# Wide matmuls in runs of one width, bank by bank, with other issue points for some transfers: a two-block transformer pass on one core

## The chip, the cores and the metric

The kernel runs on one core of a Trainium2 chip. The time is device microseconds of one launch, the median over several runs. The core has TensorE (PE), VectorE (DVE), ScalarE (ACT) and GpSimd (POOL), and SyncE (SP), which here only issues transfers.

## The reference

One sequence of 256 tokens with 2,048 channels goes through two blocks, in float32. The first has an RG-LRU branch and a sparse-attention branch in parallel, an MLP with squared ReLU and a gated projection of an embedding (PLE). The second has two layers: stick-breaking attention beside gated linear attention, then an S5 state-space mixer with a GLU, each followed by a SwiGLU feed-forward.

```python
y = concatenate([rms_norm(rglru(...)), rms_norm(nsa(...))]); h = h + rms_norm(y @ w_out)
f = square(relu(rms_norm(h) @ mlp_w1)) @ mlp_w2;             h = h + rms_norm(f)
h = h + sigmoid(h @ ple_gate) * (p @ ple_proj)
for layer in range(2):
    y = sb_gla_mixer(...) if layer == 0 else s5_mixer(...)   # s5: gelu(y) @ w_glu, split, val * sigmoid(gate)
    h = h + rms_norm(y)
    gate, up = split(rms_norm(h) @ w_ffn_in[layer]); h = h + rms_norm((silu(gate) * up) @ w_ffn_out[layer])
```

The sparse attention adds a relative position bias that is looked up by the distance of query and key, for 16 heads.

## The kernel before, in words

Activations lie transposed, channels on partitions and 256 tokens (`T`) in the free dimension. Every float32 product is made of three rounded ones: weights and activations are split into a rounded part and a rest (`wh`, `wl`; `X[:, 0]`, `X[:, 1]`), and `wh` times both parts of `X` and `wl` times the first are summed in PSUM.

`wload` (L253 to L263) fetches a weight tile of 512 KB on SyncE's queue into `wr`; ScalarE rounds it to `wh` (L261) and VectorE subtracts to get `wl` (L262). A tile holds two contraction steps `kk` by four output tiles `j` of 128 columns.

`group` (L287 to L322) runs one group: four PSUM banks, one for each `j`, and 8 or more weight tiles. In its **wide** form, each product is a matmul of 512 columns (`wh` with both parts of `X`) and one of 256 (`wl` with the first part), issued by the helper on L304. In its **narrow** form there are three of 256 columns. Stages that are wide: the MLP, the PLE gate, both feed-forwards, the GLU. Narrow ones fill the first block's and the second's mixers. Groups alternate between banks of tag `ps` only and `px, px, ps, ps` (`gpar`). `evac` (L340 to L367) empties a bank: ScalarE copies one half (L357), VectorE adds the other (L361, L364). `pre` is set for the first group of a stage, whose activations are split as it goes (L249).

The order on each engine is set by a list scheduler that goes by program order and priorities; `low(n)` shifts the priority, `issue_after` puts an instruction behind another. Side work comes from generators: `mix_step` takes two steps of `self.mix` after each weight tile in the first block, and `bg_step` takes steps of a background generator in the MLP and layer 0's feed-forward: the S5 tables are made there, much of it on GpSimd. Its `prod` (L1713) makes 32x128 matmuls (L1720), which GpSimd's work on L1762 waits for.

`bias_tables` (L595) makes the 16x511 bias table on TensorE and writes it, skewed, as a [16, 128, 256] tensor `tab` to DRAM, from 16 partitions; `bias_gen` reads it back. `s5` (L1797) loads its tables TB, TT and CBd, and `relay` (L1809) moves the Gelu outputs from one partition layout to another in eight copies per cut, cuts of 8, 4 and 4 column tiles; the issuing engines take turns. The GLU's activations are split from its result (L1948, L1949).

Of the kernel before, what the change touches and what calls it, by code (L numbers as in the profile page):

```python
# [9 lines left out]
F32 = mybir.dt.float32  # L10
# [8 lines left out]
P = 128  # L19
# [38 lines left out]
def layout(inp):  # L58
# [25 lines left out]
    rb = np.zeros((33, 16), np.float32)  # L84
    rb[:32] = g["rel_bias"]
    rb[32] = NEG
    o["relb"] = rb
    dist = np.arange(511) - 255
    b = np.where(dist >= 0, _rel_bucket(dist), 32)
    oh = np.zeros((33, 2, 511), np.float32)  # L90
    oh[b, 0, np.arange(511)] = 1.0
    oh[:, 1] = oh[:, 0, ::-1]
    o["oh"] = oh
    cst = np.zeros((P, 4, P), np.float32)
    cst[:, 0] = np.eye(P)
# [41 lines left out]
class K:  # L137
    def __init__(self, tc, I, out, es, dump=None):
        self.tc, self.nc, self.I, self.out = tc, tc.nc, I, out
        self.es = es  # L140
        self.dumpf = dump
        pool = lambda name, bufs, **k: es.enter_context(tc.tile_pool(name=name, bufs=bufs, **k))
        self.cp = pool("const", 1)
        self.xp = pool("xp", 6)
        self.wp = pool("wp", 4)
        self.ep = pool("ep", 5)
        self.mp = pool("mp", 9)
        self.sp = pool("sp", 4)
# [5 lines left out]
        self.mix, self.mix_n, self.summed = [], 1, None  # L154
        self.hold = ()

    def nm(self, s):
# [95 lines left out]
    def wload(self, pieces, shape=(P, 2, 512)):  # L253

        nc = self.nc
        wr = self.wp.tile(list(shape), F32, tag="wr", name=self.nm("wr"))
        for sl, src in pieces:
            nc.sync.dma_start(wr[sl], src)
# [28 lines left out]
    def group(self, Xk, ks, load, ntile=4, pre=None, narrow=None, tag="ps", kc=2):  # L287

        nc = self.nc
        narrow = not self.alt if narrow is None else narrow
        lhs = lambda w, kk, j: w[:, kk, j * P:(j + 1) * P]
        if narrow:
            banks = [self.ps(tag) for _ in range(ntile // 2)]
            ps = [banks[j // 2][:, (j % 2) * T:(j % 2 + 1) * T] for j in range(ntile)]
        else:
            tags = ["ps"] * 4
            if self.alt:
                self.gpar ^= 1  # L300
                tags = [["ps"] * 4, ["px", "px", "ps", "ps"]][self.gpar]
            ps = [self.ps(tags[j]) for j in range(ntile)]
        n = len(ks)
        mm = lambda o, w, x, a, z: nc.tensor.matmul(o, w, x, start=a, stop=z, skip_group_check=True)  # L304
        for c in range(0, n, kc):
            if pre:
                for k in ks[c:c + kc]:
                    pre(k)
            wh, wl = load(ks[c])
            for kk in range(kc):  # L310
                i = c + kk
                X = Xk(ks[i])
                for j in range(ntile):
                    if narrow:
                        mm(ps[j], lhs(wh, kk, j), X[:, 0], i == 0 and j % 2 == 0, False)
                        mm(ps[j], lhs(wh, kk, j), X[:, 1], False, False)
                        mm(ps[j], lhs(wl, kk, j), X[:, 0], False, i == n - 1)
                    else:
                        mm(ps[j], lhs(wh, kk, j), X, i == 0, False)
                        mm(ps[j][:, 0:T], lhs(wl, kk, j), X[:, 0], False, i == n - 1)  # L320
            self.mix_step()
        return ps  # L322

# [271 lines left out]
    def bias_tables(self):  # L595

        nc, I = self.nc, self.I
        relb = self.m([33, 16], tag="relb", bufs=1)
        nc.scalar.dma_start(relb, I["relb"])
        oh = self.wp.tile([33, 2, 511], F32, tag="wr", name="oh")  # L600
        nc.scalar.dma_start(oh, I["oh"])
        ps = self.ps()
        nc.tensor.matmul(ps[0:16, 0:511], relb, oh[:, 1], start=True, stop=True)
        tb = self.m([16, 512])
        nc.vector.tensor_copy(tb[:, 0:511], ps[0:16, 0:511])
        self.tab = self.dp.tile([16, P, T], F32, tag="tab", name="tab")
        skew = bass.AP(tensor=tb.tensor, offset=tb.offset + 127, ap=[list(tb.ap[0]), [-1, P], [1, T]])
        nc.gpsimd.dma_start(self.tab, skew)


        self.bc = self.c([P, 2, 2, 8, 16], "bc")
        nc.gpsimd.memset(self.bc[:, 0], NEG)
# [11 lines left out]
    def block1_in(self):  # L624
# [36 lines left out]
        with self.tc.issue_after(self.hold[1].ins):  # L661
            L = self.lru_open(UG)
        cmp_ = {}
        self.mix, self.mix_n = [self.compress_gen(kk, cmp_), self.bias_gen(), self.lru_gen(L)], 2

        sl = lambda a, b: (slice(None), slice(None), slice(a, b))
        ps = self.group(Xk, ks, lambda k0: self.wload([(sl(0, 256), self.wsrc(W, k0, C_KS, 2, 256)),
# [385 lines left out]
    def block1(self):  # L1053
# [24 lines left out]
            ld(k)  # L1078
        self.upd = self.post_norm(Y, acc)
        self.mlp()  # L1080
        self.ple()
        self.dump("h3", self.h)

# [387 lines left out]
    def ffn(self, layer):  # L1471
        nc, I = self.nc, self.I
        V, S = nc.vector, nc.scalar
        X, pre = self.make_x(("ng2", layer * 64 + 32))
        rb = self.rtile("a")
        W1, W2 = I["w_ffn_in_2"][layer], I["w_ffn_out_2"][layer]
        Y = self.newY()
# [41 lines left out]
    def s5_gen(self):  # L1519
# [193 lines left out]
        def prod():  # L1713

            k, cx, bt = pend
            kt = self.ps()
            for i in range(2):
                for r in range(4):
                    q = 2 * r + i
                    nc.tensor.matmul(kt[r * 32:r * 32 + 32, 0:P], bt[:, i, r * 32:r * 32 + 32],  # L1720
                                     cx[q // 4][:, q % 4].rearrange("p t h -> p (t h)"), start=(i == 0), stop=(i == 1),
                                     skip_group_check=True)
# [74 lines left out]
    def s5(self):  # L1797
        nc, I = self.nc, self.I
        V, S = nc.vector, nc.scalar

        TB = [self.xs([P, 4, 2, 16, 32], F32) for _ in range(2)]
        for kp in range(8):
            nc.sync.dma_start(TB[kp // 4][:, kp % 4], self.TBd[kp])
        U = self.xs([P, 8, NK, 32], F32)
        Us = self.xs([P, 8, NK, 32], F32)
        fl = lambda a: a.rearrange("p g k c -> p g (k c)")
# [117 lines left out]
        def outer(kp):  # L1924
# [83 lines left out]
```

## Time and profile before

| | us |
|---|---|
| median of 3 runs | 3652.32 (3651.43 to 3671.67) |
| profiled execution, device time | 3657.45 |
| its span, first to last instruction | 3655.6 |
| TensorE busy | 3501.3 |
| stages by the profile: first mixer | 0 to 449 |
| MLP | 449 to 1205 |
| PLE and second block's first mixer | 1205 to 1750 |
| feed-forward, layer 0 | 1750 to 2590 |
| S5 | 2590 to 2688 |
| GLU | 2688 to 2874 |
| feed-forward, layer 1 | 2882 to 3655 |

Times in the rows below are from the start of the span. A row of a timeline is: start, duration, engine, line, operation, output and inputs, and in brackets how long the engine was idle before it and what ended that. Matmuls are pipelined: their durations overlap, and the distance from start to start is what one costs.

### The profile page before, as it was taken

To read this page: it belongs to the slowest core of one execution; us is meant where nothing else is said; L and a number is where in the kernel's file an instruction comes from. 1 tells how busy PE (TensorE), PEld (TensorE's weight loads), DVE (VectorE), ACT (ScalarE), POOL (GpSimd) and SP (SyncE) were. 2 spreads that over 40 slices of the span, in tenths; PEclk is the share of its full clock that TensorE was granted. 3 is DMA by queue.
4 is the path that set the end of the run, shared out by engine and by line. 5 is a ranking of instruction groups with operands and counts; after the bars stand their busy time and mean duration, and the time that the engine had idled before them with its cause. 6 is when DMAs were issued, how large, how long until landed. Compare 5 with 4: busy or idle time off the path is not lost. (4 is left out here: it accounts for less than half of the span.)

```text
span 3655.6 us, 59158 instructions
## 1 busy us (share of the span) xinstructions
PE 3501.3 (96%) x22198; PEld 3060.9 (84%) x22198; DVE 2353.4 (64%) x3610; ACT 1833.1 (50%) x2879; POOL 1022.5 (28%) x1498
## 2 busy tenths in 40 slices
PE   8989999999999999999899999999779999999998
PEld 8888888888888898999787888887668888888887
DVE  6686785567656866546765566566755765555566
ACT  4656654644445654346644444344555544444444
POOL 1231242299620112104334555465400200000000
PEclk9999999999999999999999999999989999999999
DMA  8644456667765564565567776677875466665663
GB/s 216 207 130 151 130 172 189 181 210 211 229 202 187 180 198 135 149 194 187 161 207 227 225 228 211 212 225 246 261 219 185 144 192 188 190 187 188 187 187 127
DMA packets 506551, 699.60 MB, mean 191 GB/s; under 512 B 43239, under 2 KB 317671, under 8 KB 506264
## 3 DMA queue, kind: packets, MB, share of 16 engines
q1 hardware_dynamic: 472848, 628.60, 55.8%
q0 software_dynamic: 27120, 63.05, 5.8%
q10 hardware_dynamic: 6296, 4.17, 0.4%
q8 instruction: 174, 2.85, 0.3%
q14 instruction: 113, 0.93, 0.1%
HBM read 654.22 MB, written 37.22 MB: 189 GB/s over the span
## 5 line engine op out<-in xcount | busy, mean ns | idle before, releaser
L304 PE MATMUL ps<-x,wh 128*128 128x512 f32 (+1 forms) x8560 | 2498.4, 355 | 62.1 <-DVE e L361 19.3
L262 DVE TENSOR_TENSOR wl<-wr,wh 128x1024 fp32r<-128x1024 f32 x1126 | 1441.4, 1285 | 1099.6 <-ACT wh L261 1095.3
L304 PE MATMUL ps<-x,wl 128*128 128x256 f32 x6832 | 1922.4, 283 | 0.8 <-DVE wl L262 0.8
L261 ACT ACTIVATE wh<-wr 128x1024 fp32r<-128x1024 f32 x1126 | 1184.0, 1057 | 1245.0 <-PE ps L304 1051.9
L304 PEld LDWEIGHTS ps<-x,wh 128*128 128x128 f32 x8560 | 1510.7, 191 | 319.5 <-issue 30.3
L304 PEld LDWEIGHTS ps<-x,wl 128*128 128x128 f32 x6832 | 1306.1, 191 | 11.1 <-issue 5.6
L304 PE MATMUL px<-x,wh 128*128 128x512 f32 (+1 forms) x1776 | 658.3, 396 | 11.2 <-DVE x L249 6.8
L304 PE MATMUL px<-x,wl 128*128 128x256 f32 x1744 | 491.7, 282 | 0.5 <-DVE wl L262 0.5
L304 PEld LDWEIGHTS px<-x,wh 128*128 128x128 f32 x1776 | 332.6, 189 | 94.4 <-DVE x L249 8.6
L304 PEld LDWEIGHTS px<-x,wl 128*128 128x128 f32 x1744 | 330.5, 190 | 4.8 <-issue 3.2
L527 POOL TENSOR_TENSOR e<-x,r_c 128x256 f32<-128x256 f32 x40 | 39.8, 1001 | 1051.0 <-DVE r_c L448 1042.8
L357 ACT ACTIVATE e<-ps 128x256 f32<-128x256 f32 x324 | 120.5, 377 | 75.2 <-PE ps L304 63.4
L1762 POOL TENSOR_TENSOR m<-m,m 128x128 f32<-128x128 f32 x128 | 70.3, 573 | 302.5 <-PE pm L1720 302.5
L376 POOL TENSOR_TENSOR acc<-acc,sq 128x256 f32<-128x256 f32 x89 | 78.0, 876 | 252.7 <-ACT sq L375 250.0
L245 ACT ACTIVATE x<-e 128x256 fp32r<-128x256 f32 x168 | 68.2, 411 | 90.1 <-DVE e L1500 47.3
L246 DVE TENSOR_TENSOR x<-e,x 128x256 fp32r<-128x256 f32 x168 | 86.0, 521 | 26.4 <-ACT x L245 22.6
L1761 POOL TENSOR_TENSOR m<-m,m 128x128 f32<-128x128 f32 x128 | 82.7, 671 | 0.7
L1779 POOL TENSOR_TENSOR m<-m,m 128x256 f32<-128x256 f32 x64 | 59.6, 932 | 71.7 <-DMA m<-in_s5bT_dram 71.0
L361 DVE TENSOR_TENSOR e<-ps,e 128x256 f32<-128x256 f32 x168 | 69.9, 416 | 6.4 <-ACT e L357 6.4
L1780 POOL TENSOR_TENSOR m<-m,m 128x256 f32<-128x256 f32 x64 | 73.7, 1152 | 0.1
L738 PE MATMUL ps<-wh,x 128*128 128x512 f32 x160 | 64.6, 404 | 0.0
L740 PE MATMUL ps<-wh,x 128*128 128x512 f32 x160 | 63.2, 395 | 0.0
(488 smaller groups left out, 2895.3 us busy)
## 6 DMA issues: line engine op xcount, KB each, us to landing
wr<-in_w_ffn_in_dram SPq DMA_DIRECT2D x704, 256.0 KB, 3.3
wr<-in_mlp_w_dram SPq DMA_DIRECT2D x256, 512.0 KB, 4.2
wr<-in_w_ffn_out_dram SPq DMA_DIRECT2D x176, 512.0 KB, 4.3
wr<-in_w_in_dram SPq DMA_DIRECT2D x152, 512.0 KB, 3.8
wr<-in_w_out_dram SPq DMA_DIRECT2D x64, 512.0 KB, 4.1
wr<-in_w_glu_dram SPq DMA_DIRECT2D x128, 256.0 KB, 3.1
wr<-in_ple_gate_dram SPq DMA_DIRECT2D x32, 512.0 KB, 4.5
wr<-in_w_in_dram SPq DMA_DIRECT2D x32, 256.0 KB, 4.9
```

Source lines behind the costliest of these rows:

```text
L245: a = nc.scalar.activation(dst[:, 0], src, AF.Copy)
L246: b = (eng or nc.vector).tensor_tensor(dst[:, 1], src, dst[:, 0].bitcast(F32), op=ALU.subtract)
L261: nc.scalar.activation(wh, wr, AF.Copy)
L262: nc.vector.tensor_tensor(wl, wr, wh.bitcast(F32), op=ALU.subtract)
L304: mm = lambda o, w, x, a, z: nc.tensor.matmul(o, w, x, start=a, stop=z, skip_group_check=True)
L357: a = S.activation(t, ps[:, T:2 * T], AF.Copy)
L361: self.hold = a, V.tensor_tensor(y, ps[:, 0:T], t, op=ALU.add)
L376: (eng or nc.vector).tensor_tensor(acc, acc, q, op=ALU.add)
L738: nc.tensor.matmul(ps, xh, wh, start=first, stop=False, skip_group_check=True)
L1761: G_.tensor_tensor(cx[:, q], u_(0), l_(0), op=ALU.mult)
L1762: G_.tensor_tensor(t1[:, q], u_(1), l_(1), op=ALU.mult)
L1780: G_.tensor_tensor(t1, v4(gb[0][:, 1]), v4(gb[1][:, 1 - ri]), op=ALU.mult)
```

## The change

Five things change. First, `group` goes through a weight tile bank by bank (all `kk` of one `j`, then the next `j`; in a first group only its last tile) and, where it is wide, takes the products in runs: up to `self.run` matmuls with `wh`, then as many with `wl`. `self.run` is 8 up to the end of the MLP, 2 from the PLE gate through layer 0's feed-forward and the GLU, 4 in layer 1's feed-forward. Second, the bias table is made on 128 partitions (eight copies of the 16 heads) and written in eight pieces, each of 16 rows from another 16 partitions; the pieces come from a generator at the head of `self.mix`, and the table's one-hot matrix no longer lies in a weight buffer. Third, `prod`'s matmuls get a higher priority. Fourth, the S5 tables TB and two of TT are loaded in between or behind the last 25 weight loads ahead of S5. Fifth, the relay of the Gelu outputs is issued by GpSimd alone for the first cut, by GpSimd and SyncE for the other two, where GpSimd and ScalarE (and SyncE in the last) took turns.

```diff
-    o["relb"] = rb
+    o["relb"] = np.tile(rb, (1, 8))
-    oh = np.zeros((33, 2, 511), np.float32)
+    oh = np.zeros((33, 512), np.float32)
...
+        self.run = 8
...
             wh, wl = load(ks[c])
-            for kk in range(kc):
-                i = c + kk
-                X = Xk(ks[i])
-                for j in range(ntile):
-                    if narrow:
...
-                    else:
-                        mm(ps[j], lhs(wh, kk, j), X, i == 0, False)
-                        mm(ps[j][:, 0:T], lhs(wl, kk, j), X[:, 0], False, i == n - 1)
+            order = [(kk, j) for j in range(ntile) for kk in range(kc)]
+            if pre and c + kc < n:
+                order = [(kk, j) for kk in range(kc) for j in range(ntile)]
+            runs = 1 if narrow else self.run
+            for r in range(0, len(order), runs):
+                for part in range(2):
+                    for kk, j in order[r:r + runs]:
...
+                        elif part == 0:
+                            mm(ps[j], lhs(wh, kk, j), X, i == 0, False)
+                        else:
+                            mm(ps[j][:, 0:T], lhs(wl, kk, j), X[:, 0], False, i == n - 1)
...
-        relb = self.m([33, 16], tag="relb", bufs=1)
+        relb, oh = self.m([33, P], tag="relb", bufs=1), self.m([33, 512])
-        oh = self.wp.tile([33, 2, 511], F32, tag="wr", name="oh")
...
-        skew = bass.AP(tensor=tb.tensor, offset=tb.offset + 127, ap=[list(tb.ap[0]), [-1, P], [1, T]])
-        nc.gpsimd.dma_start(self.tab, skew)
+        def gen():
+
+            for r in range(8):
+                rows = tb[r * 16:r * 16 + 16]
+                nc.gpsimd.dma_start(self.tab[:, r * 16:r * 16 + 16], bass.AP(
+                    tensor=rows.tensor, offset=rows.offset + 127 - 16 * r, ap=[list(rows.ap[0]), [-1, 16], [1, T]]))
+                yield 1
+
+        self.tab_gen = gen()
...
-        self.mix, self.mix_n = [self.compress_gen(kk, cmp_), self.bias_gen(), self.lru_gen(L)], 2
+        self.mix, self.mix_n = [self.tab_gen, self.compress_gen(kk, cmp_), self.bias_gen(), self.lru_gen(L)], 2
...
         self.mlp()
+        self.run = 2
         self.ple()
...
+        self.run = (2, 4)[layer]
...
+            with self.low(-self.bg_low):
+                for i in range(2):
+                    for r in range(4):
+                        q = 2 * r + i
+                        nc.tensor.matmul(kt[r * 32:r * 32 + 32, 0:P], bt[:, i, r * 32:r * 32 + 32],
...
+        late = self.loads[-25:]
         for kp in range(8):
-            nc.sync.dma_start(TB[kp // 4][:, kp % 4], self.TBd[kp])
+            with self.tc.issue_after(late[3 * kp].ins):
+                nc.sync.dma_start(TB[kp // 4][:, kp % 4], self.TBd[kp])
...
-                nc.sync.dma_start(tl[:, i], tt_src(len(tts)))
+                with self.tc.issue_after(late[-1].ins):
+                    nc.sync.dma_start(tl[:, i], tt_src(len(tts)))
...
-                    relay(Yg, Yt, k0, k1, (nc.gpsimd, nc.scalar) if i < 2 else (nc.gpsimd, nc.scalar, nc.sync))
+                    relay(Yg, Yt, k0, k1, (nc.gpsimd, nc.sync) if i else (nc.gpsimd,))
```

On TensorE in layer 0's feed-forward (one weight tile, `wh_19239` with its rest; four banks) the order before is:

```order
L304 MATMUL px_19140<-x_18755,wh_19239 128x512
L304 MATMUL px_19140<-x_18755,wl_19240 128x256
L304 MATMUL px_19141<-x_18755,wh_19239 128x512
L304 MATMUL px_19141<-x_18755,wl_19240 128x256
L304 MATMUL ps_19142<-x_18755,wh_19239 128x512
L304 MATMUL ps_19142<-x_18755,wl_19240 128x256
L304 MATMUL ps_19143<-x_18755,wh_19239 128x512
L304 MATMUL ps_19143<-x_18755,wl_19240 128x256
L304 MATMUL px_19140<-x_18755,wh_19239 128x512
L304 MATMUL px_19140<-x_18755,wl_19240 128x256
L304 MATMUL px_19141<-x_18755,wh_19239 128x512
```

and after the change, for the same tile, which is now called `wh_19246` (x2 stands for the two contraction steps):

```order
L305 MATMUL px_19147<-x_18762,wh_19246 128x512 x2
L305 MATMUL px_19147<-x_18762,wl_19247 128x256 x2
L305 MATMUL px_19148<-x_18762,wh_19246 128x512 x2
L305 MATMUL px_19148<-x_18762,wl_19247 128x256 x2
L305 MATMUL ps_19149<-x_18762,wh_19246 128x512 x2
L305 MATMUL ps_19149<-x_18762,wl_19247 128x256 x2
L305 MATMUL ps_19150<-x_18762,wh_19246 128x512 x2
L305 MATMUL ps_19150<-x_18762,wl_19247 128x256 x2
L305 MATMUL px_19147<-x_18762,wh_19269 128x512 x2
L305 MATMUL px_19147<-x_18762,wl_19270 128x256 x2
```

The two contraction steps of a bank now stand together, two of 512 columns and then two of 256; the fourth bank is reached after six pairs of the tile and no longer after three. In the MLP all eight `wh` products of a tile stand ahead of its eight `wl` products.

On SyncE, at the end of S5, where the last CBd loads (L1794), the relay's copies (L1812, `x<-x`) and the GLU's weight loads (L258) meet, the order before is:

```order
L1794 DMA wl_27933<-CBd 128x1024
L1794 DMA wr_27943<-CBd 128x1024
L258 DMA wr_27980<-in_w_glu_dram 128x2x256 x2
L258 DMA wr_28007<-in_w_glu_dram 128x2x256 x2
L258 DMA wr_28034<-in_w_glu_dram 128x2x256 x2
L258 DMA wr_28061<-in_w_glu_dram 128x2x256
L1812 DMA x_27572<-x_27571 128x1x128 x2
L258 DMA wr_28061<-in_w_glu_dram 128x2x256
```

and after the change (L1812, L1832 and L259 are the same lines):

```order
L1812 DMA wl_27940<-CBd 128x1024
L1832 DMA x_27579<-x_27578 128x1x128 x4
L1812 DMA wr_27950<-CBd 128x1024
L259 DMA wr_27987<-in_w_glu_dram 128x2x256 x2
L259 DMA wr_28014<-in_w_glu_dram 128x2x256 x2
L259 DMA wr_28041<-in_w_glu_dram 128x2x256 x2
L259 DMA wr_28068<-in_w_glu_dram 128x2x256
L1832 DMA x_27579<-x_27578 128x1x128 x4
L259 DMA wr_28068<-in_w_glu_dram 128x2x256
```

Four copies have come in ahead of the last CBd load and four among the GLU's weight loads, where two stood before; ScalarE had eleven such copies and has none now.

## Rows read from the trace of the kernel before

**Rows 1.** the page: busy time of the engines; shares of the last chain

```profile
PE 3501.3 (96%) x22198; PEld 3060.9 (84%) x22198; DVE 2353.4 (64%) x3610; ACT 1833.1 (50%) x2879; POOL 1022.5 (28%) x1498
...
PE 36%; DVE 3%; DMA 2%; ACT 1%; issue 1%; POOL 0%; ACTq 0%; SPq 0%; DVEq 0%; POOLq 0%
```

**Rows 2.** TensorE's groups by shape: count, busy us, mean ns, idle before

```profile
L304 PE MATMUL ps<-x,wh 128*128 128x512 f32 x5104 | 1853.4, 400 | 46.6 <-DVE e L361 19.3 <-DVE x L249 13.7 <-DVE x L361 6.3
L304 PE MATMUL px<-x,wh 128*128 128x512 f32 x1712 | 646.8, 400 | 11.2 <-DVE x L249 6.8 <-ACT wh L261 2.6 <-DVE x L1949 1.8
```

**Rows 3.** windows, line 304 alone: length, PE busy (count), PEld, clock, DMA, GB/s

```profile
2950.00:3600.00 650.00, 650.00 (x3709) 565.95 (x3708) 1.00 0.61 188
3100.00:3200.00 100.00, 100.00 (x577) 87.51 (x577) 1.00 0.61 189
```

**Rows 4.** TensorE's waits over the span: us in total, times, longest

```profile
PE ps L304 <- DVE e L361: 19.3, 14, 2.9
PE ps L304 <- ACT wh L261: 14.1, 4, 7.5
```

**Rows 5.** timeline of TensorE, second mixer, 512 columns behind 512

```profile
1555.05 0.39 PE L740 MATMUL ps<-wh,x 128*128 128x512 f32 x1
...
1562.30 0.39 PE L739 MATMUL ps<-wl,x 128*128 128x512 f32 x1
```

**Rows 6.** timeline of TensorE, first mixer, narrow triples of 256 columns

```profile
60.04 0.28 PE L304 MATMUL ps<-x,wl 128*128 128x256 f32 x1
...
60.40 0.28 PE L304 MATMUL ps<-x,wl 128*128 128x256 f32 x1
```

**Rows 7.** timeline of TensorE, second mixer, 256 columns, weights of 16 columns

```profile
1371.75 0.28 PE L728 MATMUL ps<-x,wl 128*16 128x256 f32 x1
...
1372.09 0.28 PE L728 MATMUL ps<-x,wl 128*16 128x256 f32 x1
```

**Rows 8.** the page's costliest groups: a weight load, and VectorE's subtraction

```profile
L262 DVE TENSOR_TENSOR wl<-wr,wh 128x1024 fp32r<-128x1024 f32 x1126 | 1441.4, 1285 | 1099.6 <-ACT wh L261 1095.3
...
L304 PEld LDWEIGHTS ps<-x,wl 128*128 128x128 f32 x6832 | 1306.1, 191 | 11.1 <-issue 5.6
```

**Rows 9.** TensorE's waits in layer 0's feed-forward, 1760 to 2590 us

```profile
PE ps L304 <- DVE e L361: 11.8, 6, 2.9
...
PE ps L304 <- DVE x L361: 4.9, 4, 2.0
PE ps L304 <- DVE e L364: 4.8, 3, 3.4
```

**Rows 10.** TensorE's waits in the MLP, 460 to 1205 us

```profile
PE ps L304 <- DVE e L361: 7.5, 8, 1.9
```

**Rows 11.** timelines of VectorE and TensorE in layer 0's feed-forward

```profile
2250.69 3.56 DVE L262 TENSOR_TENSOR wl<-wr,wh 128x1024 fp32r<-128x1024 f32 x1 [0.43 <-ACT wh L261]
...
2256.75 0.79 PE L304 MATMUL ps<-x,wh 128*128 128x512 f32 x1 [2.52 <-DVE e L361]
```

**Rows 12.** window of all engines there; the clock follows POOL

```profile
2256.00:2260.00 4.00, 3.25 (x10) 2.78 (x11) 2.43 (x6) 2.39 (x4) 3.48 (x6) 0.57 0.52 183
```

**Rows 13.** transfers issued from 55 to 100 us: count, KB, us to landing

```profile
tab<-m POOLq DMA_DIRECT2D x1, 2048.0 KB, 25.5
wr<-in_w_in_dram SPq DMA_DIRECT2D x8, 256.0 KB, 14.4
```

**Rows 14.** timeline of TensorE, first mixer and end of S5

```profile
84.77 0.58 PE L304 MATMUL ps<-x,wh 128*128 128x256 f32 x1 [5.73 <-ACT wh L261]
...
2680.07 1.08 PE L1847 MATMUL px<-wl,x 128*32 128x128 f32 x16 [5.15 <-DMA wl<-CBd]
```

**Rows 15.** timeline of ScalarE, end of S5

```profile
2673.69 7.88 ACTq L1812 DMA_DIRECT2D x<-x  x4
2681.61 0.60 ACT L1930 ACTIVATE x<-pm 128x512 f32<-128x512 f32 x1 [7.95 <-DMA x<-x]
```

**Rows 16.** GpSimd's waits over the span

```profile
POOL m L1762 <- PE pm L1720: 302.5, 12, 86.8
```

More of the change, by code (lines that the diff above doesn't have):

```diff
@@ L86, in layout @@
     rb[32] = NEG
-    o["relb"] = rb
+    o["relb"] = np.tile(rb, (1, 8))
     dist = np.arange(511) - 255
     b = np.where(dist >= 0, _rel_bucket(dist), 32)
-    oh = np.zeros((33, 2, 511), np.float32)
-    oh[b, 0, np.arange(511)] = 1.0
-    oh[:, 1] = oh[:, 0, ::-1]
+    oh = np.zeros((33, 512), np.float32)
+    oh[b, 510 - np.arange(511)] = 1.0
     o["oh"] = oh
@@ L154, in __init__ @@
         self.mix, self.mix_n, self.summed = [], 1, None
+        self.loads = []
+        self.run = 8
         self.hold = ()
@@ L257, in wload @@
         for sl, src in pieces:
-            nc.sync.dma_start(wr[sl], src)
+            self.loads.append(nc.sync.dma_start(wr[sl], src))
         wh = self.wp.tile(list(shape), F32R, tag="wh", name=self.nm("wh"))
@@ L309, in group @@
             wh, wl = load(ks[c])
-            for kk in range(kc):
-                i = c + kk
-                X = Xk(ks[i])
-                for j in range(ntile):
-                    if narrow:
-                        mm(ps[j], lhs(wh, kk, j), X[:, 0], i == 0 and j % 2 == 0, False)
-                        mm(ps[j], lhs(wh, kk, j), X[:, 1], False, False)
-                        mm(ps[j], lhs(wl, kk, j), X[:, 0], False, i == n - 1)
-                    else:
-                        mm(ps[j], lhs(wh, kk, j), X, i == 0, False)
-                        mm(ps[j][:, 0:T], lhs(wl, kk, j), X[:, 0], False, i == n - 1)
+            order = [(kk, j) for j in range(ntile) for kk in range(kc)]
[5 more added lines that the diff above has]
+                    for kk, j in order[r:r + runs]:
+                        i = c + kk
+                        X = Xk(ks[i])
+                        if narrow and part == 0:
+                            mm(ps[j], lhs(wh, kk, j), X[:, 0], i == 0 and j % 2 == 0, False)
+                            mm(ps[j], lhs(wh, kk, j), X[:, 1], False, False)
+                        elif narrow:
+                            mm(ps[j], lhs(wl, kk, j), X[:, 0], False, i == n - 1)
+                        elif part == 0:
+                            mm(ps[j], lhs(wh, kk, j), X, i == 0, False)
+                        else:
+                            mm(ps[j][:, 0:T], lhs(wl, kk, j), X[:, 0], False, i == n - 1)
             self.mix_step()
@@ L597, in bias_tables @@
         nc, I = self.nc, self.I
-        relb = self.m([33, 16], tag="relb", bufs=1)
+        relb, oh = self.m([33, P], tag="relb", bufs=1), self.m([33, 512])
         nc.scalar.dma_start(relb, I["relb"])
-        oh = self.wp.tile([33, 2, 511], F32, tag="wr", name="oh")
         nc.scalar.dma_start(oh, I["oh"])
         ps = self.ps()
-        nc.tensor.matmul(ps[0:16, 0:511], relb, oh[:, 1], start=True, stop=True)
-        tb = self.m([16, 512])
-        nc.vector.tensor_copy(tb[:, 0:511], ps[0:16, 0:511])
+        nc.tensor.matmul(ps, relb, oh, start=True, stop=True)
+        tb = self.m([P, 512])
+        nc.vector.tensor_copy(tb, ps)
         self.tab = self.dp.tile([16, P, T], F32, tag="tab", name="tab")
-        skew = bass.AP(tensor=tb.tensor, offset=tb.offset + 127, ap=[list(tb.ap[0]), [-1, P], [1, T]])
-        nc.gpsimd.dma_start(self.tab, skew)
+        def gen():
[5 more added lines that the diff above has]
+        self.tab_gen = gen()
         self.bc = self.c([P, 2, 2, 8, 16], "bc")
@@ L1716, in prod @@
             kt = self.ps()
[L1717 to L1722, printed above, removed]
+            with self.low(-self.bg_low):
[3 more added lines that the diff above has]
+                        nc.tensor.matmul(kt[r * 32:r * 32 + 32, 0:P], bt[:, i, r * 32:r * 32 + 32],
+                                         cx[q // 4][:, q % 4].rearrange("p t h -> p (t h)"), start=(i == 0), stop=(i == 1),
+                                         skip_group_check=True)
             kp = self.m([P, 240])
```

## The prediction

> **What bounds the kernel now.** I read the page first: TensorE is busy 96% of the span, 3501 us, and the chain that ended last is TensorE's more than any other engine's [rows 1]. So the time is TensorE's instruction stream plus its holes, and a change counts only if it shortens the one or closes the other. I then asked four things of the trace: how long one product takes when nothing waits, who TensorE waits for, what happened in the largest holes, and what clock it got there.
>
> The stream is 6,816 wide pairs: a 512-column matmul with the rounded weights `wh`, then a 256-column one with their rests `wl` [rows 2]. From 2950 to 3600 us TensorE issues 3,709 line-304 matmuls in 650 us at full granted clock and without a hole: 350.5 ns a pair. In the best 100 us it is 577, or 346.6 ns a pair [rows 3]. The span holds 154 us in which TensorE is idle (3655.6 - 3501.3). The largest entries in its list of waits are VectorE's evacuation (`e L361`, 19.3 us in 14 waits) and late `wh` tiles (14.1 us in 4) [rows 4].
>
> The profiled execution has a span of 3655.6 us and took 3657.45 us by the device clock; the median of the runs is 3652.32. The sum is made against 3657.45; I carry its difference over to the median.
>
> **1. Wide products in runs.** The arithmetic stays, only the order within one weight tile changes (8 pairs a tile): eight `wh` then eight `wl` up to the end of the MLP, two and two through the gate projection, layer 0's feed-forward and the GLU, four and four in layer 1. What does a matmul cost behind one of its own width? 512 behind 512, each with its own weights: 32 instructions from 1555.05 to 1562.30 us, 226.6 ns each [rows 5]. 256 behind 256, each with its own 128-column weights: three in 0.36 us, 120 ns each [rows 6]. Together 346.6 ns, the same as the best alternating stretch. So alternation costs on average 350.5 - 346.6 = 3.9 ns a pair, and I book it to the two changes of width in a pair. A run of r keeps one of r: it saves 7/8, 1/2, 3/4 of it. By the counts in the program's order there are 1,984 pairs at r=8, 2,768 at r=2 and 2,064 at r=4: 1,736 + 1,384 + 1,548 = 4,668 pairs saved, times 3.9 ns = **-18 us**.
>
> Bounds. Not all width changes need cost something: the alternation itself drops to 346.6, so 0 is possible. Below that, 256-column matmuls with 16-column weights go at 0.34 us for three, 113.3 ns [rows 7]; if runs did that with 128-column weights, the pair saves 10.6 ns: -49 us. I do not take it, since the full-sized row is the nearer one. Above: a weight load's own record lasts 191 ns [rows 8]; were a `wl` run held to that, a pair would take 226.6 + 191 = 418 ns. The 120 ns are of this very matmul with such loads, so I stay with it and treat the rest as a rival below.
>
> [...]
>
> **2. Banks free sooner, needed sooner.** The new order goes bank by bank within a weight tile, where the old one visited all four banks for each contraction step. At the end of a group the first bank's last product therefore lies further ahead of the group's end: 1.04 us before, 0.72 at r=8, 2.08 at r=2, 1.62 at r=4 (the products that follow it, at the durations above). Evacuation can start 1 us sooner in layer 0's feed-forward. Against it, the next group reaches its third bank no earlier than before (0.9 us before, about 1.4 to 1.6 after, by position) and its fourth 0.1 to 0.6 us earlier. There TensorE waits 11.8 + 4.8 + 4.9 us for evacuations [rows 9]. [...] The 13 waits lose 0.4 to 0.9 us each where they are as long, some 6 us, and I add 3 us for half-clock spells that no longer follow: **-9 us**. Bounds: all 21.5 us and the spells, -28; or +8, if the fourth bank is now what is late. In the MLP they are 7.5 us [rows 10]; there r=8 frees the first bank later, not sooner, and the third is needed 0.2 us later: **-1** (-5..+5). Layer 1 has hardly any.
>
> **3. The bias table.** One 2 MB write from 16 partitions takes 25.5 us; beside it eight weight loads of 256 KB take 14.4 us each [rows 13], ScalarE has no tile to round, and TensorE stands still for 5.73 us [rows 14]. The change writes the same bytes in eight pieces from 16 partitions each; GpSimd issues the eight with nothing between them. Each piece still reads 16 partitions, so the crowding may last as long; what is sure is that the table's source no longer holds a weight buffer. The hole and as much clock as the stall above lost are some 8 us, and smaller holes follow: bounds 0 to -15, nearer 0 because bytes and queue stay: **-3**. The compression's matmuls and the gate work move back in this block by about 96 matmuls; they cover one another, 0 (-10..+10).
>
> **4. Relays of the S5 output.** Before, ScalarE issued half of them itself: it stood 7.88 us in one batch, and the next Gelu waited 7.95 us [rows 15]. TensorE meanwhile waited 5.15 us for CBd [rows 14]. Now GpSimd and SyncE issue them. The stall goes to SyncE: its four copies wait for the sixth Gelu and stand ahead of the last CBd load, and the GLU's weight loads are queued behind that. That Gelu is no longer held, so I put the CBd load at about its old time and the last Gelus some 3 us sooner: **-3** (-8..+3).
>
> **5. At nothing.** The `prod` matmuls (line 1720) stand some 14 us earlier in TensorE's queue; GpSimd waited 302.5 us in 12 waits for their results [rows 16], 25 us in the mean, and TensorE's list of waits has no entry for that line: GpSimd's inputs lie ready far ahead, and 14 us fit in. Were that cover gone, each of 32 rounds would hold TensorE for the missing time. The loads of TB and `ttq` are spread over, or put behind, the last weight loads of layer 0; what they take from the queue is the same bytes, read only by S5 behind that stage.
>
> **Sum:** -18 - 9 - 1 - 3 - 3 = -34: 3657.45 - 34 = 3623 by a profile like this one, **3619 us** in the terms of the median (3652.3 - 34, rounded up).
>
> **Rivals.** *The runs gain nothing* and only the holes shrink: -16, 3636 us. For it: the alternation reaches 346.6 by itself in places. Against: it does so rarely, the mean over 650 us is 350.5.
> *More than one hole closes at once:* 256-runs towards 113 ns (-30 rather than -18), the feed-forward's stalls gone (-21) and the table's hole with its clock (-10): 3652 - 61 = 3591. For it: each term's bound is a row; against: VectorE's 3.56 us operation and the table's bytes stay.
> *Weight loads set the pace of the `wl` runs.* In alternation a short matmul is followed by a long one, beside which a load has time; eight short ones in a row have none, and its record lasts 191 ns [rows 8]. The run loses from 124 ns a `wl` matmul on (350.5 - 226.6), and the kernel becomes slower by over 1% from 135 ns (36.5 us and the other terms' 16 over 4,668 pairs are 11 ns more). At 140 ns: 4,668 x 16 ns = +75, less 16: 3711 us. Against it: the narrow triples load weights for every matmul and go at 120 ns.
> [...]
>
> **Chances.** Sum as made, 3603 to 3634: 50%. More holes, below 3603: 19%, and the bare rate 1%. Runs gain nothing, 3634 to 3660: 23%. Weight loads or a new wait, above 3660: 7%, most of it above 3689. A measurement here tells about 1%, 36.5 us, from no change, so faster is below 3616: 20 plus 17 of the forecast's 50, 37%; slower 5%; within 1%: 58%. The range of 3585 to 3652 leaves out some 3% below and 15% above.
>
> **What would show it.** Step 1: line-304 matmuls in 3000 to 3100 us rising above 573, in the MLP most; like-after-like at 226 and 120. Step 2: `e L361`, `e L364` and `x L361` in layer 0's feed-forward falling from 21.5 us to about 15. Step 3: the 5.73 us hole. Step 4: no ScalarE wait for `x<-x`, and a GLU that starts 3 us sooner after the feed-forward. It is wrong if runs keep 350 ns a pair, or if the fourth bank or GpSimd's products become TensorE's wait.

## The result, and the profile after

The changed kernel takes 3609.95 us in the median, the kernel before 3654.62 beside it: the ratio is 0.9871, with a 95% interval of 0.9831 to 0.9911. The forecast was 3619 within 3585 to 3652. The profiled execution took 3605.78 us (before 3657.45); the page says of it, in the form of [rows 1]:

```profile
PE 3475.6 (96%) x22198; PEld 3054.7 (85%) x22198; DVE 2336.3 (65%) x3610; ACT 1829.6 (51%) x2880; POOL 1024.9 (28%) x1510
...
PE 82%; DVE 7%; issue 3%; ACT 3%; DMA 2%; POOL 2%; SPq 0%; ACTq 0%; DVEq 0%; POOLq 0%
```

TensorE's busy time fell by 26 us and its idle time from 154 to 128 us. Where the time went is seen by stage. I take a wide stage from the start of its first 512-column product to that of its last, by count, so that both traces are cut at the same instruction; the first mixer is what lies ahead of the MLP. Us by the profiles:

| stage | before | after | difference | forecast |
|---|---|---|---|---|
| first mixer | 449.2 | 437.1 | -12.1 | -3 |
| MLP | 741.2 | 735.7 | -5.6 | -8 |
| feed-forward, layer 0 | 804.2 | 772.7 | -31.5 | -13 |
| between it and the GLU (S5) | 124.8 | 123.6 | -1.2 | -3 |
| GLU | 160.6 | 157.2 | -3.4 | -1 |
| feed-forward, layer 1 | 732.6 | 735.3 | +2.7 | -6 |
| all else | 643.0 | 642.4 | -0.6 | -1 |

So the total came out near the forecast, from other terms. Layer 0's feed-forward gave more than twice its share, the first mixer four times, and layer 1, which should have gained 6 us, gained nothing (before + prod, below, has its old code and takes 735.2 there). TensorE's waits in layer 0's feed-forward (those of [rows 9]; L369 and L372 are the old L361 and L364):

```profile
PE ps L305 <- DVE x L250: 6.9, 6, 1.8
PE ps L305 <- ACT x L548: 2.4, 1, 2.4
PE ps L305 <- DVE x L369: 2.0, 1, 2.0
PE ps L305 <- DVE e L372: 1.1, 1, 1.1
...
PE ps L305 <- DVE e L369: 1.0, 4, 0.4
```

The three entries of evacuation are 4.1 us where they were 21.5. The table's write and the weight loads beside it, in the form of [rows 13]:

```profile
wr<-in_w_in_dram SPq DMA_DIRECT2D x16, 256.0 KB, 5.4
...
tab<-m POOLq DMA_DIRECT2D x8, 256.0 KB, 10.1
```

A weight load beside the write lands after 5.4 us where it was 14.4, and the hole of 5.73 us [rows 14] has no successor. The pair's cost in layer 1, in the form of [rows 3]:

```profile
2900.00:3550.00 650.00, 649.97 (x3698) 565.87 (x3697) 1.00 0.60 187
```

3,698 matmuls in 650 us are 351.5 ns a pair, where it was 350.5.

### The profile page after: what moved, and what is told of

It reads as the page before. It is cut to its first block, busy times and chain, and to the rows that moved or that the text cites. A ratio compares the mean times of both kernels' runs of the same rounds, so it can differ in the third digit from the quotient of the medians.

```text
span 3604.0 us, 59118 instructions
## 1 busy us (share of the span) xinstructions
PE 3475.6 (96%) x22198; PEld 3054.7 (85%) x22198; DVE 2336.3 (65%) x3610; ACT 1829.6 (51%) x2880; POOL 1024.9 (28%) x1510
## 4 chain that ended last, share of the span: by engine, by line
PE 82%; DVE 7%; issue 3%; ACT 3%; DMA 2%; POOL 2%; SPq 0%; ACTq 0%; DVEq 0%; POOLq 0%
PE ps L305 60%; PE px L305 15%; DVE wl L263 1%; ACT wh L262 1%; DVE x L536 1%; PE ps L753 1%; PE ps L755 1%; PE ps L754 1%; PE pm L1738 1%; DVE e L535 1%; DVE x L250 1%; POOL acc L384 0%; DMA wr<-in_w_in_dram 0%; PE px L975 0%; DMA m<-in_wg_dram 0%
## 5 line engine op out<-in xcount | busy, mean ns | idle before, releaser
L305 PE MATMUL ps<-x,wh 128*128 128x512 f32 (+1 forms) x8560 | 2135.8, 354 | 40.7 <-DVE x L250 15.3
L305 PEld LDWEIGHTS ps<-x,wh 128*128 128x128 f32 x8560 | 1395.0, 191 | 149.2 <-issue 18.0
L305 PE MATMUL ps<-x,wl 128*128 128x256 f32 x6832 | 1387.8, 283 | 0.0
L305 PEld LDWEIGHTS ps<-x,wl 128*128 128x128 f32 x6832 | 1182.5, 191 | 147.0 <-issue 2.4
L305 PE MATMUL px<-x,wh 128*128 128x512 f32 (+1 forms) x1776 | 523.0, 395 | 12.9 <-DVE x L250 7.3
L305 PEld LDWEIGHTS px<-x,wl 128*128 128x128 f32 x1744 | 295.1, 190 | 54.2 <-issue 2.6
L305 PEld LDWEIGHTS px<-x,wh 128*128 128x128 f32 x1776 | 291.1, 190 | 41.8 <-DVE x L250 8.6
L305 PE MATMUL px<-x,wl 128*128 128x256 f32 x1744 | 313.8, 282 | 0.0
L369 DVE TENSOR_TENSOR e<-ps,e 128x256 f32<-128x256 f32 x168 | 69.8, 417 | 2.9 <-ACT e L365 2.9
L753 PE MATMUL ps<-wh,x 128*128 128x512 f32 x160 | 64.1, 400 | 0.1
L754 PE MATMUL ps<-wl,x 128*128 128x512 f32 x160 | 62.6, 391 | 0.8 <-DVE wl L263 0.8
```

What stands on the lines that cost most here:

```text
L753: nc.tensor.matmul(ps, xh, wh, start=first, stop=False, skip_group_check=True)
L754: nc.tensor.matmul(ps, xh, wl, start=False, stop=False, skip_group_check=True)
```

## The experiments

Theory A was the prediction's own: the bank order frees banks sooner. The rivals: the runs did it (B), or the side work of S5 (C), which I had put at nothing. Most runs undo or change one thing in the changed kernel; one adds one thing to the kernel before; the last two move `prod` in the kernel with runs of 2. Us by stage from each profile, and medians:

| kernel | first mixer | MLP | layer 0 | GLU | layer 1 | median | ratio to before (95%) |
|---|---|---|---|---|---|---|---|
| before | 449.2 | 741.2 | 804.2 | 160.6 | 732.6 | 3654.62 | 1 |
| changed | 437.1 | 735.7 | 772.7 | 157.2 | 735.3 | 3609.95 | 0.9871 (0.9831 to 0.9911) |
| runs of 1 | 438.1 | 740.5 | 779.3 | 160.3 | 734.2 | 3618.98 | 0.9912 (0.9884 to 0.9940) |
| runs of 2 | 435.5 | 730.2 | 769.5 | 157.2 | 729.0 | 3592.04 | 0.9845 (0.9813 to 0.9877) |
| old bank order | 434.9 | 732.6 | 774.9 | 158.5 | 735.2 | 3611.03 | 0.9889 (0.9864 to 0.9915) |
| old side work | 437.8 | 739.4 | 803.9 | 158.6 | 735.9 | 3646.24 | 0.9988 (0.9965 to 1.0010) |
| old prod | 438.4 | 740.1 | 811.9 | 157.7 | 735.5 | 3645.59 | 0.9964 (0.9950 to 0.9978) |
| old TB, TT | 445.0 | 737.3 | 776.6 | 158.7 | 735.7 | 3619.56 | 0.9886 (0.9863 to 0.9909) |
| old table | 448.0 | 735.3 | 769.1 | 157.7 | 735.4 | 3613.87 | 0.9875 (0.9855 to 0.9895) |
| runs by part | 438.6 | 733.5 | 769.8 | 157.6 | 733.1 | 3602.75 | 0.9846 (0.9818 to 0.9874) |
| before + prod | 449.5 | 737.9 | 780.3 | 160.1 | 735.2 | 3629.21 | 0.9916 (0.9900 to 0.9932) |
| runs of 2, prod at 60 | 436.6 | 728.8 | 786.4 | 157.2 | 728.9 | 3607.61 | 0.9864 (0.9848 to 0.9879) |
| runs of 2, prod at 20 | 437.9 | 735.4 | 806.6 | 157.7 | 728.9 | 3637.32 | 0.9936 (0.9911 to 0.9960) |

The runs stand in four groups, each beside its own runs of before; a stage's time repeats within about 4 us where its code is the same, except the first mixer, which takes 434.9 to 445.0 with the new table. What moves it is mostly the granted clock: its mean in the mixer was 0.954 where it took 445.0 and 0.973 in the changed kernel, which is 20.5 and 11.9 us lost (the stage's time, times one less the mean).

**Runs of 1.** `self.run` is 1 throughout; the bank order stays.

```diff
-        self.run = 8
+        self.run = 1
```

> The changed kernel with runs of 1 in every wide stage: the bank-by-bank order within a weight tile stays, wh and wl alternate again. In the changed kernel's trace a pair costs 348.4 to 348.6 ns in layer 0's feed-forward and in the GLU (runs of 2), 349.6 in the MLP (8), 350.5 in layer 1 (4); before it was 351.4, 350.2 and 350.1. Theory A (the bank order closed layer 0's stalls, the runs of 2 gave only the pair's 2.9 ns): layer 0's feed-forward 773 + 6 = 779 us with evacuation waits as low as now (4 us), layer 1 unchanged within 2 us, total about 3617 us. Theory B (the runs closed the stalls): evacuation waits of layer 0 back at 20 us, feed-forward near 800 us, total 3640. Theory C (side transfers and the prod matmuls closed them): as A.

Layer 0 went to 779.3 as A and C had it, not to 800, with 3 us of evacuation waits: the runs had not closed the stalls. The runs as chosen gave some 9 us by the medians, 12 by the profiles.

**Runs of 2.** The same throughout with 2.

```diff
-        self.run = 8
+        self.run = 2
```

> The changed kernel with runs of 2 in every wide stage. If a run of 2 is what costs least per pair (348.5 ns) and frees the first bank 2.1 us ahead of the group's end everywhere: the MLP loses 1,984 x 1.1 = 2 us and most of its 8.4 us of evacuation waits, layer 1 2,064 x 2 = 4 us: total about 3600 us. Rival (the pair's cost goes by what else the core does in a stage, not by the run's length): MLP and layer 1 keep 349.6 and 350.5 ns a pair, only the MLP's waits fall: 3605 us.

3592 us, below both 3600 and 3605, 27 less than runs of 1 in the same group, and the best of all kernels here. MLP and layer 1 both gained, so the length matters and 2 is better than 4 or 8. The pair in layer 1, first with runs of 1, then of 2 (351.3 and 348.8 ns):

```profile
2910.00:3560.00 650.00, 649.94 (x3701) 565.54 (x3700) 1.00 0.59 187
```

```profile
2885.00:3535.00 650.00, 649.95 (x3727) 567.61 (x3726) 1.00 0.59 189
```

**Old bank order, new runs.** In the wide groups alone; the narrow ones keep the new order.

```diff
-            if pre and c + kc < n:
+            if not narrow or pre and c + kc < n:
                 order = [(kk, j) for kk in range(kc) for j in range(ntile)]
```

> The changed kernel with the old visiting order of the banks within a weight tile (contraction step by contraction step) and the new run lengths. Theory A (bank order closed the stalls of layer 0): evacuation waits there return towards 21 us, its feed-forward to 795 us or more, total about 3635 us. Theory C (side work): waits stay near 4 us, feed-forward 773 us, total 3610. In the MLP the order of a run of 8 changes only the wl half, so no more than 3 us either way.

Layer 0 took 774.9, 2 us more than changed; theory A falls.

**Old side work.** `prod` without its raised priority, the loads of TB and TT as before.

```diff
-            with self.low(-self.bg_low):
...
-            with self.tc.issue_after(late[3 * kp].ins):
-                nc.sync.dma_start(TB[kp // 4][:, kp % 4], self.TBd[kp])
+            nc.sync.dma_start(TB[kp // 4][:, kp % 4], self.TBd[kp])
...
-                with self.tc.issue_after(late[-1].ins):
```

> The changed kernel with the S5 side work as before: prod matmuls at their old priority, the loads of TB and of two TT tiles at their old places. Theory C: layer 0's feed-forward back towards 795 us and its evacuation waits towards 21 us, total about 3632 us. Theory A: feed-forward 773 to 777 us, total 3610 to 3615; GpSimd's waits for line 1720 back from 245 to 300 us without cost.

Layer 0 went back to 803.9, further than expected, and the total to 0.9988 of before: theory C holds, and in this kernel the side work carries nearly all of the gain. The next two split it.

**Old prod alone, then old TB and TT alone.** The two halves of the edit above; the first is

```diff
-            with self.low(-self.bg_low):
-                for i in range(2):
+            for i in range(2):
```

> The changed kernel with prod's matmuls at their old priority; TB and the two TT tiles loaded at the new places. With all three undone, layer 0's feed-forward went back from 773 to 804 us. Theory C1 (prod's place in TensorE's queue shifts GpSimd's rounds against VectorE's wl subtractions): feed-forward 798 to 806 us, some 22 VectorE subtractions over 2.5 us there (9 in the changed kernel), total about 3638 us. Theory C2 (the loads of TT, which wait on SyncE for TTd, hold up the weights): feed-forward 773 to 778, total about 3612 us.

> The changed kernel with the loads of TB and the two TT tiles at their old places, prod's matmuls at the new priority: the complement of the run before. C1: feed-forward 773 to 778 us, total 3610 to 3615 us. C2: 798 to 806 us, total about 3638.

811.9 and 776.6: it is `prod`. The 22 stretched subtractions that C1 expected did not come: over 2.5 us there are 7 in layer 0 with old `prod` and 5 in the changed kernel. The evacuation waits in layer 0, with old `prod`:

```profile
PE ps L305 <- DVE e L369: 16.2, 8, 3.1
...
PE ps L305 <- DVE x L369: 4.8, 3, 2.1
PE ps L305 <- DVE e L372: 1.6, 1, 1.6
```

and with old TB and TT:

```profile
PE ps L305 <- DVE e L372: 5.1, 3, 2.9
PE ps L305 <- DVE x L369: 2.6, 1, 2.6
PE ps L305 <- DVE e L369: 0.7, 2, 0.4
```

The second kernel's median is 10 us above changed, of which layer 0 shows 4; its first mixer, with the same code, is 8 us longer (by the clock, as above), and the intervals of the two ratios overlap, so what the moved loads are worth is not settled.

**Before, with the new place of prod alone.** The edit above, the other way round, in the kernel before.

> The kernel before with one edit: prod's matmuls at the new priority. In TensorE's order they then stand at the first pair of a group of 64 (in layer 0's feed-forward), before at the 41st. Theory C1: GpSimd waits for them and then works some 15 us; from the 41st pair that stretch lies over the group's end, where VectorE must evacuate, from the first pair it ends before it. Then this edit alone takes layer 0's feed-forward from 804 to 775 us or so and its evacuation waits from 21 to under 6 us, total about 3622 us. If it needs the bank order too: feed-forward 785 to 800, total 3635 to 3650.

Layer 0 fell from 804.2 to 780.3 and the whole by 30 us (0.9916), a little short of the expected 775 and 3622, with 8.4 us of evacuation waits where under 6 were expected. The edit is enough by itself:

```profile
PE ps L304 <- DVE e L364: 4.5, 4, 2.3
PE ps L304 <- DVE x L361: 3.3, 2, 2.6
...
PE ps L304 <- DVE e L361: 0.6, 2, 0.4
```

**Prod at pair 60 and at pair 20 of 64.** Changed, runs of 2 throughout, and in the first kernel (half as much delay again as in the kernel before, 150 for 100)

```diff
-            with self.low(-self.bg_low):
+            with self.low(self.bg_low // 2):
```

and `-self.bg_low // 2` in the second (half of the old delay).

> The changed kernel with runs of 2 everywhere (3592 us, layer 0's feed-forward 769.5) and prod's matmuls at half the old delay: in most groups they stand at pair 60 of 64. C1: GpSimd's first additions fall on the group's end, 1.4 us behind, so evacuation waits come back, 12 to 20 us, feed-forward 785 to 800, total 3608 to 3623. If only 'earlier than the 41st pair' counts, or the group's end is not what matters: below 775 and 3598.

> As the run before, but prod's matmuls at half the new advance: they stand at pair 20 of 64, and the group's end is 15 us behind, where GpSimd's stretch fades out. C1: waits between the two, 5 to 12 us, feed-forward 772 to 785, total 3595 to 3608. If earlier is all that counts: as pair 0 or 40 by half, 786.

Pair 60 gave 786.4, in the expected range, with 11.5 us of waits, a little under the 12 to 20 expected. Pair 20 gave 806.6 and 23.5 us of waits, as bad as pair 40, where I had expected the middle (5 to 12 us of waits). The waits, for pair 60 and for pair 20:

```profile
PE ps L305 <- DVE e L369: 7.1, 10, 1.2
...
PE ps L305 <- DVE e L372: 4.2, 5, 2.3
...
PE ps L305 <- DVE x L369: 0.2, 1, 0.2
```

```profile
PE ps L305 <- DVE e L369: 12.9, 13, 2.2
PE ps L305 <- DVE e L372: 6.3, 4, 4.9
...
PE ps L305 <- DVE x L369: 4.3, 3, 1.9
```

So it is not how early `prod` comes, and theory C1 as I had it is not the whole either. Layer 0 in parts, us, from the traces: TensorE's idle time, what the granted clock takes (as above), and what the 12 products of `prod` in this stage take of TensorE's stream (first to last of their matmuls, less the wide pairs between; before + prod has one product at a clock of 0.59):

| kernel | layer 0 | idle | clock | `prod` itself |
|---|---|---|---|---|
| before | 804.2 | 26.8 | 8.5 | 37.2 |
| before + prod | 780.3 | 13.0 | 5.1 | 35.8 |
| changed | 772.7 | 10.8 | 5.1 | 33.1 |
| old prod | 811.9 | 34.2 | 18.8 | 37.3 |
| runs of 2 | 769.5 | 11.0 | 1.7 | 33.1 |
| runs of 2, prod at 60 | 786.4 | 16.7 | 1.7 | 40.8 |
| runs of 2, prod at 20 | 806.6 | 25.8 | 1.7 | 50.0 |

The first way in which the place acts is `prod` itself. A product is sixteen matmuls, which the scheduler puts between the wide ones in up to eight places (here for pair 20):

```profile
2347.64 0.41 PE L1736 MATMUL pm<-m,m 128*32 128x128 f32 x2
2347.97 0.39 PE L305 MATMUL ps<-x,wl 128*128 128x256 f32 x1
2348.20 0.40 PE L305 MATMUL ps<-x,wh 128*128 128x512 f32 x1
2348.53 0.41 PE L1736 MATMUL pm<-m,m 128*32 128x128 f32 x2
2348.86 0.50 PE L305 MATMUL ps<-x,wh 128*128 128x512 f32 x1
```

A product costs 4.17 us in eight places, 3.12 in six, 2.58 in five and 1.72 in three, about 0.5 us a place. At pair 20 all twelve stand in eight places, at the first pair in five or six. Of the 37 us that pair 20 loses against runs of 2, 17 are this, and of the 17 us at pair 60, 8; of the 39 us of old `prod` only 4. So pair 60's 786.4 was in the range partly by luck.

The second way is GpSimd, which waits for `prod` and then works. With old `prod`, at the 41st pair of a group (the start, the end of a first stretch of arithmetic, and the start of a second):

```profile
2234.96 1.53 POOL L1779 TENSOR_TENSOR m<-m,m 128x128 f32<-128x128 f32 x4 [28.23 <-PE pm L1737]
...
2259.90 0.76 POOL L1798 TENSOR_TENSOR m<-m,m 128x256 f32<-128x256 f32 x1
...
2270.93 0.76 POOL L1763 TENSOR_TENSOR m<-m,s5rp 128x128 f32<-128x128 f32 x2 [8.52 <-DMA m<-in_s5cb_dram]
```

and in the changed kernel, at the first:

```profile
2196.01 1.85 POOL L1780 TENSOR_TENSOR m<-m,m 128x128 f32<-128x128 f32 x4 [26.55 <-PE pm L1738]
...
2221.01 0.86 POOL L1799 TENSOR_TENSOR m<-m,m 128x256 f32<-128x256 f32 x1
...
2229.80 0.97 POOL L1764 TENSOR_TENSOR m<-m,s5rp 128x128 f32<-128x128 f32 x2 [6.01 <-DMA m<-in_s5cb_dram]
```

Additions and multiplications go on for 26 us behind the product; GpSimd then waits 6 to 9 us for its next loads and works again from some 34 to 44 us behind it. The next two group ends come some 8 and 30 us behind a product at the 41st pair, 14 and 37 behind one at pair 20, at once and 22 behind one at pair 60, and 21.5 and 44 behind one at the first pair, where both stretches are running out. Beside GpSimd's arithmetic VectorE's `wl` subtractions stretch: in layer 0 of the kernel before, the 136 `wl` subtractions without any such work over them take 1.21 to 1.23 us, the 121 others 1.53 us in the mean and up to 3.57 [rows 11]; why they stretch, no run shows. The evacuations themselves (L361, L364) take 0.41 to 0.43 us in any case; they stand behind those.

That is most of it in the kernel before, where 13.0 of 20.3 us of evacuation waits (counted up to layer 0's last 512-column product) stand within 20 us behind a product. It is not with old `prod` in the changed kernel (8.8 of 22.7), nor at pair 20 (4.0 of 18.6) or pair 60 (2.8 of 11.2): there most waits stand at the second group end. With old `prod` and at pair 20 half of all the waits or more, 13.2 and 9.3 us, come within 7 us behind a wait of ScalarE for a late weight load. With old `prod`:

```profile
2393.16 1.06 ACT L262 ACTIVATE wh<-wr 128x1024 fp32r<-128x1024 f32 x1 [2.67 <-DMA wr<-in_w_ffn_in_dram]
...
2398.11 0.73 PE L305 MATMUL ps<-x,wh 128*128 128x512 f32 x2 [2.93 <-DVE e L369]
```

No VectorE operation of the 9 us before this wait is stretched by over 0.3 us; ScalarE's part of the evacuation stands behind the late rounding, and ahead of that GpSimd's own loads and stores run, with the DMA engines busy throughout (a share of 1.03 to 1.05 from 2386 to 2390 us). In the changed kernel ScalarE waits 21.7 us for weight loads in layer 0 too, but none of these waits lies within 7 us ahead of an evacuation wait. So the single edits show that the place of `prod` decides; that it does so by where GpSimd's round (arithmetic and transfers) meets the groups' ends fits the traces at all four places; how much of the waits goes by stretched VectorE operations and how much by late loads, no run separates.

**Old table.** The table made and written as before.

```diff
-        relb, oh = self.m([33, P], tag="relb", bufs=1), self.m([33, 512])
+        oh = self.wp.tile([33, 2, 511], F32, tag="wr", name="oh")
...
+        nc.gpsimd.dma_start(self.tab, skew)
```

> The changed kernel with the bias table made and written as before (one write of 2 MB from 16 partitions, the one-hot matrix in a weight buffer). The first mixer took 449.2 us before and 437.1 in the changed kernel. If the write crowds the weight loads: a hole of 4 to 6 us near 85 us and half clock behind it, mixer back at 447 to 450, total 3620 to 3622. Rival (the other order of tiles, compression and gates made the 12 us): mixer stays at 437 to 440, total 3610.

The first mixer is back at 448.0; the three kernels with the old table have 448.0 to 449.5 there, the ten others of the table 434.9 to 445.0. The transfers, and a hole of the old kind:

```profile
tab<-m POOLq DMA_DIRECT2D x1, 2048.0 KB, 25.3
wr<-in_w_in_dram SPq DMA_DIRECT2D x8, 256.0 KB, 14.9
```

```profile
82.27 0.80 PE L306 MATMUL ps<-x,wh 128*128 128x256 f32 x2 [3.49 <-ACT wh L263]
```

By the medians the old table costs only 4 us, since layer 0 came out 4 us shorter in this kernel: it idles as long there as the changed kernel (10.4 and 10.8 us) but loses 1.7 us to the clock instead of 5.1. By its own stage it costs 11.

**Runs by part.** Layer 1 with runs of 1, 8 and 2 in its three parts.

```diff
+            if layer:
+                self.run = {0: 1, 16: 8, 32: 2}[k_lo]
```

> The changed kernel with runs of 1, 8 and 2 in the three parts of layer 1's feed-forward (16, 16 and 12 column tiles), so that one trace shows the pair's cost at three lengths in the same stage, under the same loads. Prediction's step 1: 350.5 ns at 1, 347.1 at 8, 348.6 at 2, and like behind like at 226.6 and 120 ns. What the changed kernel's other stages suggest instead: 351, 349.7 and 348.4 ns, 512 behind 512 at 231 to 233.5. Total 3607 to 3611 us either way.

From first to last 512-column product of a part's gate and up products, by count (in the first part from its second wide group on): 352.3 ns at 1, 350.3 at 8 and 348.4 at 2. The total, 3602.75 us, lies below both forecasts. A whole run of 8 (start, then four matmuls of one kind to a row where x4 stands):

```profile
3272.13 1.09 PE L305 MATMUL px<-x,wh 128*128 128x512 f32 x4
3273.06 1.07 PE L305 MATMUL ps<-x,wh 128*128 128x512 f32 x4
3273.97 0.64 PE L305 MATMUL px<-x,wl 128*128 128x256 f32 x4
3274.44 0.64 PE L305 MATMUL ps<-x,wl 128*128 128x256 f32 x4
3274.92 1.09 PE L305 MATMUL px<-x,wh 128*128 128x512 f32 x4
```

The first four `wh` products take 0.93 us (232 ns each), the next four 0.91, the `wl` products 0.47 and 0.48 (120 each). In the mean over the 44 unbroken runs of these gate and up products, the first five `wh` products take 234.1, 235.4, 228.7, 232.3 and 230.5 ns, and only the last three 226.7; the first `wl` takes 114, the others 119 to 120. Runs of 2, where two pairs take 0.70 us or less:

```profile
3377.54 0.63 PE L305 MATMUL ps<-x,wh 128*128 128x512 f32 x2
3378.01 0.39 PE L305 MATMUL ps<-x,wl 128*128 128x256 f32 x2
3378.23 0.63 PE L305 MATMUL ps<-x,wh 128*128 128x512 f32 x2
```

**Kept weights.** Layer 1's gate and up products use one weight tile per part; the other loads, roundings and subtractions are left out.

```diff
+                    if not layer or not kept:
+                        kept[:] = self.wload([...])
```

> The kernel with runs of 1, 8 and 2 in the three parts of layer 1's feed-forward, where the gate and up products of each part use one weight tile over and over (15 of 16 loads, their rounding and subtraction left out, so the output is not the reference's). It measures what a pair costs with TensorE nearly alone. If other engines' and transfers' traffic makes a pair dearer than 346.6: 340 to 347 ns at all lengths. If the cost lies in TensorE's own alternation of widths: 350 at 1, 346.6 or less at 8. If it is TensorE's own whatever the order: 351, 350 and 348.4 as under load. Time of layer 1 otherwise as with runs by block, 733 us less what the pairs save.

A single run, 3597.9 us. With the transfers idle and VectorE's share down from 60% to 18% a pair costs 350.9 ns at 1 and 348.9 at 8 (by the same count as above; at 2 it is 350.2, where two weight tiles lose 0.37 us each and the others go at 348.4). The windows of the parts with 1 and 8:

```profile
2870.00:3000.00 130.00, 130.00 (x743) 112.76 (x742) 23.89 (x60) 17.27 (x48) 0.00 (x0) 1.00 0.00 1
3110.00:3280.00 170.00, 170.00 (x973) 149.02 (x972) 27.25 (x70) 21.45 (x57) 0.00 (x0) 1.00 0.00 1
```

Hence at 1 and 8 the pair's cost is TensorE's own to within 1.4 ns, and the slow start of a run is there too (233.3, 235.8, 228.3, 232.5, 230.8, then 226.7).

## Why the prediction was right or wrong

**Right in total, with the terms wrong.** The direction and 34 of the 45 us were forecast; which steps made them was not. That the total came near is luck: the runs and the banks were booked too large by 13 to 17 us together, the table too small by 8, and `prod`, booked at nothing, brought 24 or more.

**Step 1, the runs.** The rows were true: like behind like goes at 226.6 and 120 ns, but only from the sixth 512-column product on. What failed is the step that books the 3.9 ns to the two changes of width and lets a run of r pay them once instead of r times: behind eight `wl` products the first five `wh` products together lose 28 ns, against which the alternation's `wl` are quicker than 120 (116.6 in the mean from 2950 to 3600 us of the kernel before). Runs of 8 and 4 thus end where runs of 1 are, within 2 ns, and layer 1 did not gain its 6 us. Runs of 2 save 2.5 to 4 ns, more than the 1.95 booked. Of -18 us came 9 to 12.

**Step 2, the banks.** The bank order's -9 us is 1 to 2 us (old bank order; within the noise of 4). The stalls that it should have shortened did go, for another reason. The 3 us counted in it for half-clock spells no run shows as the bank order's: what the clock took in layer 0 fell from 8.5 to 5.1 us in the changed kernel, and to the same 5.1 in before + prod, which has the old order.

**Step 5, the moved products.** This is the step that failed most. I asked whether GpSimd would be late for its inputs and whether TensorE would wait for GpSimd, found slack on both, and booked nothing. (I also wrote of 32 rounds; there are 16 products, 12 of them in layer 0.) The slack was there: GpSimd still waits 245 us for `prod`. What I had at nothing is where GpSimd's round behind the product, its arithmetic and its transfers, falls against the groups' ends, and in how many places the product itself breaks up the wide matmuls: 24 us in layer 0 in the kernel before, 39 in the changed one, 30 to 36 by the medians. With the 24 us the parts (9 to 12 for the runs, 11 for the table) make up the 45; the 39 are more because with the new runs old `prod` left more idle time (34.2 us, not 26.8) and lost more to the clock (18.8 us, not 8.5). The rows that would have told it were there: I had shown the stretched subtraction [rows 11] and wrote that it stays, without asking what GpSimd did beside it, and I had shown that GpSimd's work is released by `prod`, after some 25 us of waiting each time [rows 16], which the new order moves by 40 pairs.

**Step 3, the table.** That the write delays the weight loads was right (14.4 us to landing where they now take 5.4), the size was not: -11 us in its stage where -3 was booked. I had reasoned that eight pieces crowd as one; a piece landed after 10.1 us, and the weight loads beside them came in 5.4. The clock that I counted beside the hole is some 3 us: over the first 100 us its mean was 0.97 before and with the old table, 1.00 in the changed kernel.

**Step 4, the relays.** ScalarE no longer stands in front of a Gelu:

```profile
2624.19 0.60 ACT L1951 ACTIVATE x<-pm 128x512 f32<-128x512 f32 x1 [1.95 <-PE pm L1879]
2626.73 0.60 ACT L1951 ACTIVATE x<-pm 128x512 f32<-128x512 f32 x1 [1.95 <-PE pm L1879]
```

It is SyncE that now stands, for the 3.07 us of its four copies, and the last CBd load is issued behind them:

```profile
2624.81 3.07 SPq L1832 DMA_DIRECT2D x<-x  x4
2627.98 0.53 SPq L1812 DMA_DIRECT2D wr<-CBd  x1
2628.61 5.18 SPq L259 DMA_DIRECT2D wr<-in_w_glu_dram  x7
```

TensorE waits 5.01 us for it, where it waited 5.15 and once more 1.85:

```profile
2632.28 1.08 PE L1867 MATMUL px<-wr,x 128*32 128x128 f32 x16 [5.01 <-DMA wr<-CBd]
```

The stage gained 1.2 us where 3 were booked; the relay was not tried alone.

**The rivals.** *The runs gain nothing* is out: with runs of 1 the kernel takes 9 us more. *Weight loads set the pace* is out: in the runs of 8 a `wl` product took 120 ns, and 124 is where the loss would begin. No run shows the bare rate that has 1% of the chances: the mean pair of a part did not fall below 348 ns. *More than one hole closes at once* was the nearest to what happened, but with the runs' part missing.

## What to carry to other kernels

When a change moves an instruction that another engine waits for, ask not only whether it comes in time but what the freed engine does next, its transfers included, and over which of the critical engine's helpers that work then falls; a place that repeats with the group's period is good or bad for every round at once. Ask also whether its instructions stay together, or break up another engine's stream. Cost measured in a steady run holds for the steady part only: try the shortest run first, here two, before longer ones.

## What the runs showed of the hardware that I had not expected

Behind eight 256-column matmuls, 512-column ones need five to get to their steady 226.7 ns; the cost before that, 228 to 236 ns, is there with the transfers idle as well. What in TensorE does it stays open. Each place at which `prod`'s matmuls (32 columns of weights) break up the wide ones costs about 0.5 us (a product 1.72 us in three places, 4.17 in eight). One write from 16 partitions took 25.3 to 25.5 us, the same bytes in eight pieces from 16 partitions each 10.1 us a piece, and only beside the first did weight loads on another queue land late, after 14.4 to 14.9 us and not 5.4.
